# Scratch in DRAM as separate tiles, and the token-sum stores moved from SP's queue to GpSimd's, in a decoder trunk kernel

## The chip, the cores and the metric

The kernel runs on one core of a Trainium2 chip. The metric is the device time of one execution in microseconds (us); lower is better. The core's engines are TensorE (PE: matmuls and transposes), VectorE (DVE), ScalarE (ACT), GpSimd (POOL) and SyncE (SP, which here only issues transfers). Each engine works through its own instructions in the order in which the program issued them. A transfer (DMA) is issued from the queue of SP, ScalarE or GpSimd and runs on the core's 16 DMA engines; an instruction that touches its data waits for it by a semaphore.

## The reference

Two layers on 2048 tokens of width 1024, in float32. Only what the kernel's stages need is shown.

```python
def even_layer(h, positions, w_in, conv_w, conv_b, gn, w_out):
    q, k, v, g_ret, cb, cc, cx, g_conv = split_cols(h @ w_in, EVEN_SPLITS)
    ...
    r = retention(q, k, v)
    r = rms_norm(r, gn.reshape(RET_HEADS, RET_DV)).reshape(b, s, RET_V)
    y_conv = cb * short_conv(cc * cx, conv_w, conv_b)
    mix = jnp.concatenate([r * jax.nn.silu(g_ret), y_conv * jax.nn.silu(g_conv)], axis=-1)
    return mix @ w_out

def odd_layer(h, positions, w_in, q_a_norm, w_qb, kv_a_norm, w_kvb, w_out):
    cq, ckv, k_rope, gate = split_cols(h @ w_in, ODD_SPLITS)
    ...
    o = causal_mla_attention(q_nope, q_rope, k_nope, k_rope, v)
    return (o.reshape(b, s, MLA_V) * jax.nn.silu(gate)) @ w_out

def reference(x, positions, pre_norm, post_norm, ...):
    h = x
    for layer in range(DEPTH):
        u = rms_norm(h, pre_norm[layer])
        y = even_layer(u, ...) if layer % 2 == 0 else odd_layer(u, ...)
        h = h + rms_norm(y, post_norm[layer])
    return h
```

## The kernel before

The large products (input projection of the even layer, its output projection, the gate of the odd layer) are done by a fast matrix algorithm: a 2 x 2 block product becomes seven products P1 to P7 whose operands are blocks or sums of blocks. Each product is one **slot**: 12 matmuls on TensorE (three per 128 rows, on high and low parts of float32 numbers), about 2.7 us. Blocks are numbered by Q, seven slots each; Q from RQ=32 on is the convolution's input, from CE=64 on the output projection, from YE=80 on the gate.

The order of the work is written out by hand, slot by slot. In slot t the program issues: the small TensorE jobs of that slot (transposes) whose PSUM results are copied out at the slot's end; then `prep`, which loads a product's stationary operand eight slots ahead into a ring of nine tiles `us` (SP's queue), rounds it five slots ahead (ScalarE, line 327) and forms the low part four slots ahead (VectorE, line 335); then the list of events that were entered for the slot with `at(slot, f)`, in the order of their entry; then ScalarE's copies of the product's PSUM. Nothing is reordered later, so the place of an event in a slot is its place in its engine's queue.

Moving operands stand in wider tiles `u` (c4T and c4B by the program's names for the tiles that they lie in): `comb_dma` loads them (SP, line 348 for blocks from ub2_d, whose name in the trace is ub_d), `comb_split` rounds and splits them (ScalarE line 363, VectorE line 364).

Sums of blocks and other intermediate results lie in DRAM scratch tensors: one tensor each, whose first index is a token half, a head, a group of weights or a block of tokens. mix_d holds the mixed rows: index 0 the retention heads (stored by ScalarE), index 1 the convolution channels (stored by GpSimd, line 960, from a tile that the trace calls j). ms_d, gs_d, ws_d, s_d hold sums of four blocks, formed in two tiles jc (load by SP at line 424, four GpSimd operations, store by SP). tu_d and ub2_d hold the normed tokens of the odd layer, as sums and as blocks, for the gate's products.

The stage that the change touches runs beside the second half of the output projection. Tokens come in eight pairs w of tiles of 128, tA = 2w (even) and tB = 2w+1 (odd). A pair begins at slot n, and the next pair begins seven slots later, so two pairs overlap. For each tile (tB first, tA two slots later): `y_rstd` (ScalarE's sum of squares, then yss on GpSimd, lines 1048 and 1049), `y_h` (VectorE: h = x + normed y), `h_out` (GpSimd's store of h_d, line 1058), `y_rstd` again, `y_u2` (VectorE: yu, line 1061), `y_tr` (TensorE's eight transposes, up_tr, line 1071; ScalarE's copies of them into uo[h], line 1079, with two stores to ub2_d from ScalarE's queue, line 1080). Then for the pair: `y_sum` (four GpSimd subtractions in place in the two tiles uo, line 1090, two at slot n+13 and two at n+14), and `t_out`: four stores of a half of uo each to tu_d, in the order T3, T2 (these read uo[1]), T1, T4 (these read uo[0]), by SP at slot n+15 (line 1096). There is one tile uo for even and one for odd tokens, so the next pair's copies overwrite what the subtractions and stores read. `x_in` (SP, line 1099) loads x into the tile that h_out reads.

The events are entered in this loop:

```python
for t, o in ((tB, 0), (tA, 2)):
    ...
    at(n + 5 + o, lambda t=t: h_out(t))
    at(n + 6 + o, lambda t=t: y_rstd(t, 1, yb["x"][t % 2]))
    at(n + 7 + o, lambda t=t: y_u2(t))
    small(n + 9 + o, *y_tr(t))
for i in range(4):
    at(n + 13 + i // 2, lambda w=w, i=i: y_sum(w, i))
at(n + 15, lambda w=w: t_out(w))
```

Slot n+14 of a pair is slot n+7 of the next one, in which that one's h_out of its even tile is entered behind it.

Of the kernel before, what the change touches and what calls it, by code (L numbers as in the profile page):

```python
# [20 lines left out]
P = 128  # L21
# [43 lines left out]
def body(ctx, tc, x, positions, pre_norm, post_norm, w_heads, w_conv, even_conv_w, even_conv_b, ret_gn,  # L65
# [37 lines left out]
    ty_d = dram.tile([2, P, 4, 4, 512], F32, name="ty_d")  # L103
    wo_d = dram.tile([2, 2, 2, P, 4, 512], F32, name="wo_d")
    ms_d = dram.tile([16, P, 4, 512], F32, name="ms_d")
    gs_d = dram.tile([4, P, 4, 512], F32, name="gs_d")
    wg_d = dram.tile([8, 2, P, 512], F32, name="wg_d")
# [4 lines left out]
    a_d = dram.tile([8, P, 4, 512], F32, name="a_d")  # L112
    s_d = dram.tile([8, P, 4, 512], F32, name="s_d")
    wt_d = dram.tile([4, P, 4, 4, 384], F32, name="wt_d")
    uc_d = dram.tile([2, P, 4, 4, 512], F32, name="uc_d")
    wh_d = dram.tile([HR, 2, P, 1536], F32, name="wh_d")
    wc_d = dram.tile([32, 2, P, 512], F32, name="wc_d")
    ws_d = dram.tile([16, P, 4, 512], F32, name="ws_d")

# [63 lines left out]
    with ExitStack() as es:  # L183
# [96 lines left out]
        def mix_rows(q_, kh, t):  # L280
            return mix_d[q_, t, kh].rearrange("p k t -> p (k t)")

        def item_dma(n_):
            if n_ >= len(SEQ) or SEQ[n_] is None:
                return
            Q, p_ = SEQ[n_]
            i = LOF[p_]
            if Q < 8:
                return
            t_ = ring_tile(n_)  # L290
            ring[n_] = t_
            L = f32(t_[:, 1])
            if Q < RQ:
                u = Q % 8
                src = a_d[u, :, AIX[i]] if i in AIX else s_d[u, :, (SIX0 if u < 2 else SIX)[i]]
                SP.dma_start(flat(L), src)
            elif Q >= YE:
                c2 = (Q - YE) % 4
                if i in AIX:
                    r, kh = divmod(AIX[i], 2)  # L300
                    SP.dma_start(flat(L), wg_d[2 * c2 + r, kh])
                else:
                    SP.dma_start(flat(L), gs_d[c2, :, SIX0[i]])
            elif Q >= CE:
                q_, w = divmod(Q - CE, 8)
                if i in AIX:
                    r, kh = divmod(AIX[i], 2)
                    SP.dma_start(flat(L), mix_rows(q_, kh, 2 * w + r))
                else:
                    SP.dma_start(flat(L), ms_d[Q - CE, :, SIX0[i]])  # L310
            else:
                g, ct, w = CQ[Q - RQ]
                if i in AIX:
                    r, kh = divmod(AIX[i], 2)
                    SP.dma_start(flat(L), wc_d[COFF[w][r] * 8 + ct, kh])
                else:
                    SP.dma_start(flat(L), ws_d[2 * ct + w, :, SIX0[i]])

# [19 lines left out]
        def comb_dma(G_, n_):  # L338
            comb_new(G_, n_)
            for H, L, k0, nk in comb[G_][n_]:  # L340
                L = f32(L)
                if n_ in TIX:
                    src = (wt_d[G_] if G_ < 4 else uc_d[G_ - 4] if G_ < 6 else ty_d[G_ - 6] if G_ < 8 else tu_d[G_ - 8])[:, TIX[n_]]
                    SP.dma_start(flat(L), src[:, k0:k0 + nk].rearrange("p k c -> p (k c)"))
                elif G_ > 5:
                    j, h = int(n_[1]) - 1, int(n_[2]) - 1
                    src = wo_d[G_ - 6, j, h] if G_ < 8 else ub2_d[G_ - 8, h, j]
                    SP.dma_start(flat(L), src[:, k0:k0 + nk].rearrange("p k c -> p (k c)"))
                elif G_ < 4:
                    SP.dma_start(flat(L), wh_d[2 * G_ + int(n_[2]) - 1, int(n_[1]) - 1])  # L350
                else:
                    j, tb = int(n_[1]) - 1, 2 * (G_ - 4) + int(n_[2]) - 1
                    for uu in range(2):
                        for c in range(2):
                            o = (2 * uu + c) * P
                            SP.dma_start(L[:, :, o:o + P], a_d[2 * tb + uu, :, 2 * c + j, k0 * P:(k0 + nk) * P].rearrange("p (k c) -> p k c", k=nk))

# [55 lines left out]
        def job(kind, a, b, t_):  # L413
# [28 lines left out]
            def store():  # L442
                if kind in "wmg":
                    dst = {"w": ws_d, "m": ms_d, "g": gs_d}[kind]
                    SP.dma_start(dst[a].rearrange("p z c -> p (z c)"), t_.rearrange("p z c -> p (z c)"))
                elif kind == "y":
                    SP.dma_start(ty_d[a, :, :, b, :], t_)
                elif kind == "r":
                    SP.dma_start(wt_d[a, :, :, b, :], t_)
                else:  # L450
                    SP.dma_start(uc_d[a, :, :, b, :], t_)

# [11 lines left out]
        with ExitStack() as rs_:  # L464
# [175 lines left out]
            def mix_tr(v, pt):  # L640
                lo = 0 if v[0] is not None else 2
                hi = 4 if v[1] is not None else 2
                mxo = bp.tile([P, 4, P], F32, tag="mxo", bufs=1, name=f"mxo{v[0]}_{v[1]}")
                A.copy(mxo[:, lo:hi], pt[:, lo:hi, :])
                for i, s in enumerate(v):
                    if s is not None:
                        h, u = units[s]
                        A.dma_start(mix_d[0, 2 * u:2 * u + 2, h // 4, :, h % 4, :].rearrange("c p t -> p c t"), mxo[:, 2 * i:2 * i + 2])

# [125 lines left out]
            for hp in range(1, 4):  # L775
                for i, (h, j) in enumerate(((2 * hp, 0), (2 * hp, 1), (2 * hp + 1, 1))):
                    at(T0(8 * hp) - 40 + 6 * i, lambda h=h, j=j: SP.dma_start(wh_d[h, j], w_heads[h, j]))
            for q_ in range(16):
                g_, ct, w = CQ[q_]
                o0, o1 = (o * 8 + ct for o in COFF[w])  # L780
                at(T0(RQ + q_) - 25, lambda o0=o0: SP.dma_start(wc_d[o0], w_conv[o0]))
                at(T0(RQ + q_) - 22, lambda o1=o1: SP.dma_start(wc_d[o1, 1], w_conv[o1, 1]))

# [138 lines left out]
            def conv_engine(t_):  # L922
# [3 lines left out]
                if j < 5:  # L926
# [24 lines left out]
                    else:  # L951
# [111 lines left out]
            def y_tr(t):  # L1063
# [40 lines left out]
            for w in range(8):  # L1104
# [31 lines left out]
        with ExitStack() as cs_:  # L1136
# [31 lines left out]
    with ExitStack() as oes:  # L1168
# [26 lines left out]
        with ExitStack() as es:  # L1195
# [4 lines left out]
            with ExitStack() as es1:  # L1200
# [645 lines left out]
```

## Time and profile before

| | before |
|---|---|
| median of 3 runs (lowest to highest) | 3025.8 us (3025.24 to 3029.86) |
| profiled execution, its time and its span | 3029.42 us, 3027.6 us |
| TensorE busy | 2929.0 us (97%) |
| VectorE, ScalarE, GpSimd busy | 1998.2 (66%), 1506.9 (50%), 1112.2 us (37%) |
| mean granted TensorE clock | 0.99 |
| moved by DMA | 592.50 MB, mean 196 GB/s |
| of that by the hardware queues q1 and q10, and the software queue q0 | 496.89 MB, 28.08 MB, 64.50 MB |

The span is the time from the first to the last instruction of the profiled execution; the time of that execution is taken around it. Busy time is the sum of an engine's instructions, without those that only issue transfers from SP and ScalarE. A wait is idle time of an engine just before an instruction, put down to what released it last ("<- DVE yu" was released by VectorE's instruction that wrote yu). Engine names with a q (SPq, ACTq, PEld for TensorE's weight loads) stand for a queue of their own.

### The profile page before, as it was taken

What the parts mean: (1) busy time and instruction counts of PE and PEld (TensorE: products, weight loads), DVE (VectorE), ACT (ScalarE), POOL (GpSimd) and SP (SyncE); (2) the same over time, 40 slices, a digit from 0 to 9 for tenths busy, and PEclk for the clock granted to TensorE, in tenths of its full rate; (3) what the DMA queues carried; (4) which work ended last, traced back from release to release, by engine and by line L of the source; (5) the groups of instructions that cost most, each with busy time, mean ns of one, the idle gap of its engine ahead of it and who ended that gap; (6) DMA issues with size and microseconds to landing.
All of it is one profiled execution on the core that took longest, in us unless ns stands there. A gap on an engine that the chain in (4) does not pass through costs nothing.

```text
span 3027.6 us, 47252 instructions
## 1 busy us (share of the span) xinstructions
PE 2929.0 (97%) x16137; PEld 2568.8 (85%) x16137; DVE 1998.2 (66%) x3713; ACT 1506.9 (50%) x3596; POOL 1112.2 (37%) x1379
## 2 busy tenths in 40 slices
PE   7989999999999999999998899999999999999999
PEld 6878989898888888878886678988899999999887
DVE  7767777867565766684687754577666666666643
ACT  5645555556333533353565653333655555555521
POOL 5554454521442044534265400023333333334210
PEclk9999999999999999999999999999999999999999
DMA  7466777756887688799999875146111212211552
GB/s 294 164 241 204 235 250 249 245 166 202 300 301 235 208 303 293 267 335 308 345 294 315 278 246 153 58 159 207 59 61 60 66 53 62 63 59 58 171 169 89
DMA packets 364993, 592.50 MB, mean 196 GB/s; under 512 B 35568, under 2 KB 209280, under 8 KB 357248
## 3 DMA queue, kind: packets, MB, share of 16 engines
q1 hardware_dynamic: 292752, 496.89, 50.4%
q0 software_dynamic: 19184, 64.50, 5.9%
q10 hardware_dynamic: 52816, 28.08, 3.1%
q8 instruction: 128, 2.10, 0.3%
q14 instruction: 113, 0.93, 0.1%
HBM read 404.80 MB, written 213.65 MB: 204 GB/s over the span
## 4 chain that ended last, share of the span: by engine, by line
PE 82%; DMA 6%; DVE 3%; POOL 3%; ACT 2%; issue 2%; SPq 0%; ACTq 0%; POOLq 0%; DVEq 0%
PE bx L87 8%; PE bx L88 7%; PE bx L89 7%; PE fy L1788 5%; PE by L87 4%; PE by L88 4%; PE by L89 4%; PE T L1593 4%; PE o L1623 2%; PE o L1622 2%; PE o L1621 2%; PE S L1540 2%; PE S L1543 2%; PE S L1544 2%; PE S L1541 2%
## 5 line engine op out<-in xcount | busy, mean ns | idle before, releaser
L335 DVE TENSOR_TENSOR us<-us 128x512 fp32r<-128x512 f32 x560 | 463.0, 833 | 58.5 <-ACT us L327 55.6
L327 ACT CAST us<-us 128x512 fp32r<-128x512 f32 x560 | 338.3, 620 | 162.8 <-DMA us<-s_d 27.2
L1561 POOL TENSOR_SCALAR P<-P,al 128x512 f32<-128x512 f32 (+2 forms) x320 | 220.1, 698 | 353.6 <-DVE al L1566 168.9
L1551 ACT ACTIVATE P<-S,nm 128x512 f32<-128x512 f32 (+2 forms) x320 | 201.0, 628 | 197.6 <-DVE nm L1548 175.5
L1548 DVE TENSOR_REDUCE nm<-S 128x1 f32<-128x512 f32 (+2 forms) x320 | 194.2, 608 | 70.9 <-PE S L1544 43.0
L402 ACT COPY u<-bx 128x512 f32<-128x512 f32 (+1 forms) x172 | 94.1, 547 | 293.5 <-PE bx L89 293.0
L408 POOL TENSOR_TENSOR jc<-jc 128x512 f32<-128x512 f32 x138 | 198.6, 1439 | 39.6 <-DMA jc<-in_even_w_out 18.0
L1597 DVE TENSOR_TENSOR TL<-T,TH 128x512 fp32r<-128x512 f32 x224 | 154.3, 689 | 63.7 <-ACT TH L1596 62.6
L1621 PE MATMUL o<-TH,vH 128*128 128x256 f32 x576 | 185.3, 322 | 0.0
L1593 PE MATMUL T<-ident,P 128*128 128x128 f32 x1088 | 166.1, 273 | 0.0
L1623 PE MATMUL o<-TH,vL 128*128 128x256 f32 x576 | 162.7, 283 | 0.0
L1622 PE MATMUL o<-TL,vH 128*128 128x256 f32 x576 | 162.2, 282 | 0.0
L87 PE MATMUL bx<-c4T,us 128*128 128x512 f32 x384 | 150.5, 392 | 2.8 <-ACT u L402 2.0
L88 PE MATMUL bx<-c4T,us 128*128 128x512 f32 x384 | 149.7, 390 | 1.5 <-DVE c4T L364 1.5
L89 PE MATMUL bx<-c4T,us 128*128 128x512 f32 x384 | 149.5, 389 | 0.0
L1596 ACT CAST TH<-T 128x512 fp32r<-128x512 f32 x224 | 131.3, 586 | 24.1 <-PE T L1593 18.8
L1593 PEld LDWEIGHTS T<-ident,P 128*128 128x128 f32 x1088 | 125.1, 140 | 7.8
L1540 PE MATMUL S<-kH,aqn 128*128 128x512 f32 (+2 forms) x320 | 118.4, 370 | 0.1
L1543 PE MATMUL S<-K,aqr 128*128 128x512 f32 (+2 forms) x320 | 115.5, 361 | 0.0
L1541 PE MATMUL S<-kL,aqn 128*128 128x512 f32 (+2 forms) x320 | 115.3, 360 | 0.0
L1544 PE MATMUL S<-K,aqr 128*128 128x512 f32 (+2 forms) x320 | 115.2, 360 | 0.0
L1542 PE MATMUL S<-kH,aqn 128*128 128x512 f32 (+2 forms) x320 | 115.0, 359 | 0.0
(525 smaller groups left out, 9253.0 us busy)
## 6 DMA issues: line engine op xcount, KB each, us to landing
us<-ws_d SPq DMA_DIRECT2D x128, 256.0 KB, 4.7
us<-s_d SPq DMA_DIRECT2D x96, 256.0 KB, 5.0
us<-wc_d SPq DMA_DIRECT2D x96, 256.0 KB, 4.8
us<-a_d SPq DMA_DIRECT2D x72, 256.0 KB, 4.8
jc<-mix_d SPq DMA_DIRECT2D x64, 256.0 KB, 5.7
ms_d<-jc SPq DMA_DIRECT2D x16, 1024.0 KB, 6.8
us<-ms_d SPq DMA_DIRECT2D x64, 256.0 KB, 6.0
qn_d<-qn POOLq DMA_DIRECT2D x32, 512.0 KB, 3.4
```

What stands on the lines that cost most here:

```text
L87: PE.matmul(o, ah, bh, start=first, stop=False, **kw)
L88: PE.matmul(o, ah, bl, start=False, stop=False, **kw)
L89: PE.matmul(o, al, bh, start=False, stop=last, **kw)
L327: A.copy(ring[n_][:, 0], f32(ring[n_][:, 1]))
L335: V.tensor_tensor(out=t_[:, 1], in0=src, in1=f32(t_[:, 0]), op=ALU.subtract)
L408: sub = lambda o, a, b: (lambda: G.tensor_tensor(out=t_[:, o], in0=t_[:, a], in1=t_[:, b], op=ALU.subtract))
L1551: later(D_EXP, lambda: A.activation(p_[:, 0:w], sp[:, 0:w], AF.Exp, bias=nm[:, j:j + 1], accum_out=sm[:, j:j + 1]))
L1561: G.tensor_scalar(t_[:, 0:ww], t_[:, 0:ww], al[:, jj:jj + 1] if n > 1 else al[:, 5:6], al[:, 5:6] if n > 1 else 1.0, op0=ALU.mult, op1=ALU ...
L1593: PE.transpose(tp[:, e, z, :], src, ident)
L1621: PE.matmul(hold[i], vH[h][:, kb, :], pth[:, c], start=first, stop=False)
L1622: PE.matmul(hold[i], vH[h][:, kb, :], ptl[:, c], start=False, stop=False)
L1623: PE.matmul(hold[i], vL[h][:, kb, :], pth[:, c], start=False, stop=last)
```

## The change

Fifteen kinds of scratch tensor that were one DRAM tile with a leading index become a Python list of DRAM tiles, one for each value of that index; sizes, layouts within a part, and the transfers' shapes are the same. In addition `t_out` issues its four stores from GpSimd's queue instead of SP's, and is entered one slot earlier, at n+14, which puts it behind the last two subtractions and ahead of the next pair's h_out. The other tensors (a_d, s_d, wt_d, uc_d, wh_d, ws_d, wo_d, wg_d, gs_d, ty_d) are changed as the ones shown.

```diff
-    mix_d = dram.tile([2, NT, 2, P, 4, P], F32, name="mix_d")
+    mix_d = [dram.tile([NT, 2, P, 4, P], F32, name=f"mix_d{i}") for i in range(2)]
...
-    ub2_d = dram.tile([2, 2, 2, P, 4, 512], F32, name="ub2_d")
-    tu_d = dram.tile([2, P, 4, 4, 512], F32, name="tu_d")
+    ub2_d = [dram.tile([2, 2, P, 4, 512], F32, name=f"ub2_d{i}") for i in range(2)]
+    tu_d = [dram.tile([P, 4, 4, 512], F32, name=f"tu_d{i}") for i in range(2)]
...
-    ms_d = dram.tile([16, P, 4, 512], F32, name="ms_d")
+    ms_d = [dram.tile([P, 4, 512], F32, name=f"ms_d{i}") for i in range(16)]
...
-    wc_d = dram.tile([32, 2, P, 512], F32, name="wc_d")
+    wc_d = [dram.tile([2, P, 512], F32, name=f"wc_d{i}") for i in range(32)]
...
-                    SP.dma_start(flat(L), ms_d[Q - CE, :, SIX0[i]])
+                    SP.dma_start(flat(L), ms_d[Q - CE][:, SIX0[i]])
...
-                            G.dma_start(mix_d[1, n0:n0 + 4, ct // 4, :, ct % 4, :].rearrange("c p t -> p c t"), ah.rearrange("p (c t) -> p c t", c=4))
+                            G.dma_start(mix_d[1][n0:n0 + 4, ct // 4, :, ct % 4, :].rearrange("c p t -> p c t"), ah.rearrange("p (c t) -> p c t", c=4))
...
-                        A.dma_start(ub2_d[half, h, j][:, :, w * P:(w + 1) * P], uo[:, j * 512:(j + 1) * 512].rearrange("p (k t) -> p k t", k=4))
+                        A.dma_start(ub2_d[half][h, j][:, :, w * P:(w + 1) * P], uo[:, j * 512:(j + 1) * 512].rearrange("p (k t) -> p k t", k=4))
...
-                    SP.dma_start(tu_d[half, :, TIX[n_], :, w * P:(w + 1) * P], src.rearrange("p (k t) -> p k t", k=4))
+                    G.dma_start(tu_d[half][:, TIX[n_], :, w * P:(w + 1) * P], src.rearrange("p (k t) -> p k t", k=4))
...
-                at(n + 15, lambda w=w: t_out(w))
+                at(n + 14, lambda w=w: t_out(w))
```

## Rows read from the trace of the kernel before

**Rows 1.** windows: length, busy PE PEld DVE ACT POOL, clock, DMA share, GB/s

```profile
...
700.00:1300.00 600.00, 599.75 (x2678) 495.26 (x2677) 384.07 (x526) 241.85 (x439) 219.24 (x190) 1.00 0.81 267
1540.00:1720.00 180.00, 156.98 (x708) 125.25 (x707) 141.48 (x139) 113.31 (x260) 105.82 (x114) 0.97 0.93 310
...
```

**Rows 2.** waits of TensorE, 1540 to 1780: total us, times, longest

```profile
...
PE up_tr L1071 <- DVE yu L1061: 6.6, 4, 2.5
PE by L88 <- DVE c4B L364: 5.2, 1, 5.2
PE bx L87 <- ACT u L402: 4.9, 3, 2.6
...
```

**Rows 3.** waits of SP's queue, 1540 to 1730: total us, times, longest

```profile
...
SPq L1096 <- POOL uo L1090: 20.5, 16, 3.2
...
SPq L1096 <- POOL yss L1048: 16.1, 5, 4.5
SPq L348 <- DMA ub_d<-uo: 11.7, 3, 6.3
...
SPq L1099 <- DMA h_d<-yx: 6.8, 4, 2.2
...
```

**Rows 4.** timeline of POOL, 1590 to 1609: start, us, operation, idle before

```profile
...
1591.23 2.66 POOL L1090 TENSOR_TENSOR uo<-uo 128x512 f32<-128x512 f32 x2 [3.65 <-DMA ub_d<-uo]
...
1594.77 2.94 POOL L1090 TENSOR_TENSOR uo<-uo 128x512 f32<-128x512 f32 x2
1597.65 0.63 POOL L1058 DMA_DIRECT2D h_d<-yx  x1
...
1600.31 0.56 POOL L1049 TENSOR_TENSOR yss<-yss,nhalf 128x1 f32<-128x1 f32 x1
...
```

**Rows 5.** timelines of VectorE and TensorE, two stretches each, columns as above

```profile
...
1600.90 1.78 DVE L1061 TENSOR_SCALAR yu<-yx,yss 128x1024 f32<-128x1024 f32 x1 [0.73 <-POOL yss L1049]
...
1603.04 0.60 PE L1071 MATMUL up_tr<-ident,yu 128*128 128x128 f32 x4
...
1646.86 1.78 DVE L1061 TENSOR_SCALAR yu<-yx,yss 128x1024 f32<-128x1024 f32 x1 [0.73 <-POOL yss L1049]
...
1650.63 0.60 PE L1071 MATMUL up_tr<-ident,yu 128*128 128x128 f32 x4
...
```

**Rows 6.** timelines of ScalarE, 1590 to 1609 and 1640 to 1680

```profile
...
1597.37 1.14 ACT L1079 ACTIVATE uo<-up_tr,gcol 128x128 f32<-128x128 f32 x4 [5.51 <-PE up_tr L1071]
...
1603.72 1.15 ACT L1079 ACTIVATE uo<-up_tr,gcol 128x128 f32<-128x128 f32 x4
1605.54 0.52 ACTq L1080 DMA_DIRECT2D ub_d<-uo  x1
...
1653.74 1.05 ACT L363 CAST u<-u 128x1024 fp32r<-128x1024 f32 x1 [4.64 <-DMA u<-ub_d]
...
```

**Rows 7.** tensor mix_d over the span: ns min/median/max, first and last start

```profile
...
L424 SPq DMA_DIRECT2D jc<-mix_d x64: 319/432/2905, 1109.5 to 1456.5; - x64
...
L960 POOL DMA_DIRECT2D mix_d<-j x32: 750/770/1017, 756.8 to 1345.3; - x32
...
```

**Rows 8.** timelines of SP's queue, 1590 to 1609 and 1640 to 1657

```profile
...
1593.91 4.18 SPq L1096 DMA_DIRECT2D tu_d<-uo  x4
...
1603.28 0.33 SPq L1099 DMA_DIRECT2D yx<-in_x  x1
...
1639.88 4.19 SPq L1096 DMA_DIRECT2D tu_d<-uo  x4
...
1644.71 0.83 SPq L348 DMA_DIRECT2D u<-ub_d  x1
...
```

**Rows 9.** DMA issues: count, KB each, median us from issue to landing

```profile
...
mix_d<-j POOLq DMA_DIRECT2D x32, 256.0 KB, 5.6
...
tu_d<-uo SPq DMA_DIRECT2D x32, 256.0 KB, 2.8
...
```

**Rows 10.** line 960: all its DMAs, min/median/max us from issue to landing

```profile
...
DMA to landing us min/median/max: 3.4/5.6/9.2
```

More of the change, by code (lines that the diff above doesn't have):

```diff
@@ L97, in body @@
     dram = ctx.enter_context(tc.tile_pool(name="dram", bufs=1, space=DRAM))
-    mix_d = dram.tile([2, NT, 2, P, 4, P], F32, name="mix_d")
+    mix_d = [dram.tile([NT, 2, P, 4, P], F32, name=f"mix_d{i}") for i in range(2)]
     h_d = dram.tile([S, D], F32, name="h_d")
     yp_d = dram.tile([S, D], F32, name="yp_d")
-    ub2_d = dram.tile([2, 2, 2, P, 4, 512], F32, name="ub2_d")
-    tu_d = dram.tile([2, P, 4, 4, 512], F32, name="tu_d")
-    ty_d = dram.tile([2, P, 4, 4, 512], F32, name="ty_d")
-    wo_d = dram.tile([2, 2, 2, P, 4, 512], F32, name="wo_d")
-    ms_d = dram.tile([16, P, 4, 512], F32, name="ms_d")
-    gs_d = dram.tile([4, P, 4, 512], F32, name="gs_d")
-    wg_d = dram.tile([8, 2, P, 512], F32, name="wg_d")
+    ub2_d = [dram.tile([2, 2, P, 4, 512], F32, name=f"ub2_d{i}") for i in range(2)]
+    tu_d = [dram.tile([P, 4, 4, 512], F32, name=f"tu_d{i}") for i in range(2)]
+    ty_d = [dram.tile([P, 4, 4, 512], F32, name=f"ty_d{i}") for i in range(2)]
+    wo_d = [dram.tile([2, 2, P, 4, 512], F32, name=f"wo_d{i}") for i in range(2)]
+    ms_d = [dram.tile([P, 4, 512], F32, name=f"ms_d{i}") for i in range(16)]
+    gs_d = [dram.tile([P, 4, 512], F32, name=f"gs_d{i}") for i in range(4)]
+    wg_d = [dram.tile([2, P, 512], F32, name=f"wg_d{i}") for i in range(8)]
     gate_d = dram.tile([D, S], F32, name="gate_d")
@@ L111, in body @@
     qr_d = dram.tile([HM, P, S], F32, name="qr_d")
[L112 to L116, printed above, removed]
-    wc_d = dram.tile([32, 2, P, 512], F32, name="wc_d")
-    ws_d = dram.tile([16, P, 4, 512], F32, name="ws_d")
+    a_d = [dram.tile([P, 4, 512], F32, name=f"a_d{i}") for i in range(8)]
+    s_d = [dram.tile([P, 4, 512], F32, name=f"s_d{i}") for i in range(8)]
+    wt_d = [dram.tile([P, 4, 4, 384], F32, name=f"wt_d{i}") for i in range(4)]
+    uc_d = [dram.tile([P, 4, 4, 512], F32, name=f"uc_d{i}") for i in range(2)]
+    wh_d = [dram.tile([2, P, 1536], F32, name=f"wh_d{i}") for i in range(HR)]
+    wc_d = [dram.tile([2, P, 512], F32, name=f"wc_d{i}") for i in range(32)]
+    ws_d = [dram.tile([P, 4, 512], F32, name=f"ws_d{i}") for i in range(16)]
     const = ctx.enter_context(tc.tile_pool(name="const", bufs=1))
@@ L280, in mix_rows @@
         def mix_rows(q_, kh, t):
-            return mix_d[q_, t, kh].rearrange("p k t -> p (k t)")
+            return mix_d[q_][t, kh].rearrange("p k t -> p (k t)")
         def item_dma(n_):
@@ L294, in item_dma @@
                 u = Q % 8
-                src = a_d[u, :, AIX[i]] if i in AIX else s_d[u, :, (SIX0 if u < 2 else SIX)[i]]
+                src = a_d[u][:, AIX[i]] if i in AIX else s_d[u][:, (SIX0 if u < 2 else SIX)[i]]
                 SP.dma_start(flat(L), src)
@@ L300, in item_dma @@
                     r, kh = divmod(AIX[i], 2)
-                    SP.dma_start(flat(L), wg_d[2 * c2 + r, kh])
+                    SP.dma_start(flat(L), wg_d[2 * c2 + r][kh])
                 else:
-                    SP.dma_start(flat(L), gs_d[c2, :, SIX0[i]])
+                    SP.dma_start(flat(L), gs_d[c2][:, SIX0[i]])
             elif Q >= CE:
@@ L314, in item_dma @@
                     r, kh = divmod(AIX[i], 2)
-                    SP.dma_start(flat(L), wc_d[COFF[w][r] * 8 + ct, kh])
+                    SP.dma_start(flat(L), wc_d[COFF[w][r] * 8 + ct][kh])
                 else:
-                    SP.dma_start(flat(L), ws_d[2 * ct + w, :, SIX0[i]])
+                    SP.dma_start(flat(L), ws_d[2 * ct + w][:, SIX0[i]])
         def item_hi(n_):
@@ L346, in comb_dma @@
                     j, h = int(n_[1]) - 1, int(n_[2]) - 1
-                    src = wo_d[G_ - 6, j, h] if G_ < 8 else ub2_d[G_ - 8, h, j]
+                    src = wo_d[G_ - 6][j, h] if G_ < 8 else ub2_d[G_ - 8][h, j]
                     SP.dma_start(flat(L), src[:, k0:k0 + nk].rearrange("p k c -> p (k c)"))
                 elif G_ < 4:
-                    SP.dma_start(flat(L), wh_d[2 * G_ + int(n_[2]) - 1, int(n_[1]) - 1])
+                    SP.dma_start(flat(L), wh_d[2 * G_ + int(n_[2]) - 1][int(n_[1]) - 1])
                 else:
@@ L355, in comb_dma @@
                             o = (2 * uu + c) * P
-                            SP.dma_start(L[:, :, o:o + P], a_d[2 * tb + uu, :, 2 * c + j, k0 * P:(k0 + nk) * P].rearrange("p (k c) -> p k c", k=nk))
+                            SP.dma_start(L[:, :, o:o + P], a_d[2 * tb + uu][:, 2 * c + j, k0 * P:(k0 + nk) * P].rearrange("p (k c) -> p k c", k=nk))
         def comb_split(G_, n_, half, sub=V):
@@ L446, in store @@
                 elif kind == "y":
-                    SP.dma_start(ty_d[a, :, :, b, :], t_)
+                    SP.dma_start(ty_d[a][:, :, b, :], t_)
                 elif kind == "r":
-                    SP.dma_start(wt_d[a, :, :, b, :], t_)
+                    SP.dma_start(wt_d[a][:, :, b, :], t_)
                 else:
-                    SP.dma_start(uc_d[a, :, :, b, :], t_)
+                    SP.dma_start(uc_d[a][:, :, b, :], t_)
             return [load] + job_ops(t_, kind) + [store]
@@ L647, in mix_tr @@
                         h, u = units[s]
-                        A.dma_start(mix_d[0, 2 * u:2 * u + 2, h // 4, :, h % 4, :].rearrange("c p t -> p c t"), mxo[:, 2 * i:2 * i + 2])
+                        A.dma_start(mix_d[0][2 * u:2 * u + 2, h // 4, :, h % 4, :].rearrange("c p t -> p c t"), mxo[:, 2 * i:2 * i + 2])
             NU = len(units)
@@ L776, in body @@
                 for i, (h, j) in enumerate(((2 * hp, 0), (2 * hp, 1), (2 * hp + 1, 1))):
[L777 removed]
+                    at(T0(8 * hp) - 40 + 6 * i, lambda h=h, j=j: SP.dma_start(wh_d[h][j], w_heads[h, j]))
             for q_ in range(16):
@@ L781, in body @@
                 at(T0(RQ + q_) - 25, lambda o0=o0: SP.dma_start(wc_d[o0], w_conv[o0]))
-                at(T0(RQ + q_) - 22, lambda o1=o1: SP.dma_start(wc_d[o1, 1], w_conv[o1, 1]))
+                at(T0(RQ + q_) - 22, lambda o1=o1: SP.dma_start(wc_d[o1][1], w_conv[o1, 1]))
             x_load(0)
@@ L811, in t_op @@
                     V.tensor_tensor(out=raw0[o][:, c], in0=raw0[a_][:, c], in1=raw0[b_][:, c], op=ALU.subtract)
-                SP.dma_start(wt_d[0, :, TIX[n_]].rearrange("p k c -> p (k c)"), raw0[o])
+                SP.dma_start(wt_d[0][:, TIX[n_]].rearrange("p k c -> p (k c)"), raw0[o])
             rope_pos(psb)
@@ L1155, in body @@
                     if (ct % 2, kh) != (1, 0):
-                        at(T0(CE) + 2 + 7 * ct + kh, lambda ct=ct, kh=kh: SP.dma_start(wg_d[ct, kh], w_gate[ct, kh]))
+                        at(T0(CE) + 2 + 7 * ct + kh, lambda ct=ct, kh=kh: SP.dma_start(wg_d[ct][kh], w_gate[ct, kh]))
             at(T0(CE) + 6, y_open)
@@ L1225, in u_dma @@
                         w = (t % 8) // 2
-                        SP.dma_start(urr[t][:, 4 * j:4 * j + 4, :], ub2_d[t // 8, t % 2, j][:, :, w * P:(w + 1) * P])
+                        SP.dma_start(urr[t][:, 4 * j:4 * j + 4, :], ub2_d[t // 8][t % 2, j][:, :, w * P:(w + 1) * P])
                 def u_split(t):
```

2 lines of the change are left out of this document (1 added, 1 removed).

## The prediction

> **What bounds the kernel now.** I read the page first: TensorE is busy 97% of the span, so time comes or goes only where TensorE waits, or is made to. The table by stretches says where that is [rows 1]. From 700 to 1300 us TensorE is busy 599.75 us of 600, though the DMA engines are busy 0.81 of the time there; from 1540 to 1720, the stage in which the changed stores lie, it is busy 156.98 us of 180, at a granted clock of 0.97 and a DMA share of 0.93. So 23 us of idling stand in that stage, and the reader is to see that nothing is idle where most of the split tiles (mix_d, ws_d, wc_d, a_d) are at work.
>
> The table of waits tells what TensorE waits for in the stage [rows 2]. The largest is the transposes of a normed tile (up_tr, line 1071) waiting for VectorE's last scaling (yu, line 1061): 6.6 us in four waits. Then two sorts that belong to the combined operand tiles loaded in the same slots: 5.2 us for c4B, 4.9 us for ScalarE's copies of u (line 402). The rest is smaller.
>
> Then SP's queue, which issues every operand load [rows 3]: in front of the four token-sum stores (line 1096) it stood 20.5 us in 16 waits for GpSimd's subtractions, and 16.1 us in 5 more. The loads queued behind were late by as much. That is what the move to GpSimd takes off SP, and the case for it.
>
> Last, timelines of one pair of token tiles, engine by engine, to see in which order the work goes. GpSimd subtracts twice at 1591.23 and twice at 1594.77, then at once issues the hidden-state store h_d at 1597.65 in 0.63 us, and has at 1600.31 the small power (yss) that VectorE's scaling of 1600.90 is waiting for [rows 4, 5]. TensorE transposes its result at 1603.04, 0.36 us after the scaling's end at 1602.68. ScalarE copies the other tile's transposes out at 1597.37, this one's at 1603.72 to 1604.87, and issues the store of its halves at 1605.54 [rows 6]; the next pair's first subtractions wait for such a store.
>
> **Part 1: the split of the scratch tensors.** It takes away a wait only if a load now waits for a store to another index of the same tensor. mix_d is the test: its loads (line 424) begin at 1109.5 us while stores of line 960 to the other half go on to 1345.3 [rows 7]. With a wait on the whole tensor the first load would have come after the last of these. Sizes, shapes and numbers of the transfers stay. So 0, and no work is needed to hide it. Below it, what a freed wait could be worth at most is the 11.7 us that SP waits for a store of ub_d in this stage [rows 3]: a load there reads the very pair that was stored, so I expect it to stay. Above it, nothing is added.
>
> **Part 2a: four DMA issues on GpSimd, in front of the next pair's work.** A pair's four stores are now issued after its fourth subtraction, ahead of h_out and of the yss of the next pair's even tile, in GpSimd's order. The nearest row is a GpSimd store of the same size and shape, mix_d from j: 750 to 1017 ns of the engine, median 770 [rows 7]; four are 3.08 us (3.0 to 4.1). yss, VectorE's scaling and the transposes come that much later; behind the scaling VectorE has its operand splits, and behind the transposes TensorE has its main products. What covers it is the slack at the transposes: 0.36 us in the pair shown, from 1602.68 to 1603.04. Of the six pairs that run in this loop four look like that (slack 0.35, 0.36, 0.36, 0.61) and two like the one at 1640: the scaling ends at 1648.64, the transposes begin at 1650.63, slack 1.99 (the other 2.28) [rows 5]. So TensorE is stopped for 2.5 + 3 x 2.7 + 1.1 + 0.8 = 12.5 us over the stage.
>
> **Part 2b: the stores land later, and ScalarE waits for them.** A store reads half of the tile that ScalarE fills next. T3 is now issued by SP at 1593.91, right after the first two subtractions, and is over when ScalarE starts at 1597.37 [rows 6, 8]. Moved behind all four subtractions it can't start before 1597.65, and ScalarE must wait until it has landed. SP's stores of tu_d land 2.8 us after the issue; GpSimd's of the same size land after a median of 5.6, 3.4 at the least and 9.2 at the most [rows 9, 10]. I take 4.2, midway between 2.8 and 5.6: the destination is that of the SP row, the queue that of the other. ScalarE's copy starts 1597.65 + 4.2 − 1597.37 = 4.5 us late. The slack that eats it is that before its stores: the copies of the even tile end at 1604.87, the store is issued at 1605.54, 0.67 us [rows 6]; in the four early pairs this is 0.67, 2.06, 0.67 and 0.75. The lateness passes from there round the loop: store, next pair's subtractions, yss, scaling, transposes. This is the same path as 2a's, so the greater of the two counts in each pair: 4.0 − 0.67 = 3.3, 2.7 (2a's), 4.5 − 0.67 = 3.8, 4.5 − 0.75 = 3.7 (the first pair's start of copies lies 0.2 us after its subtractions, the others' 0.3 before). The last two pairs have ScalarE late for other reasons, so 2a's 1.1 and 0.8 stay. The sum is 15.4 us. With 2.8 us to landing only 2a is left, 12.5; with 9.2 the four pairs cost about 8 to 9 each, some 35 in all.
>
> **Part 2c: what SP gains.** SP no longer stands from 1593.91 to 1598.09 in line 1096, nor in the wait ahead of it; loads behind go out sooner. In the later pairs one of them matters: u from ub_d was issued at 1644.71 right behind the stores that ended at 1644.07, and ScalarE waited 4.64 us for it [rows 6, 8]. TensorE's own 4.9 us of waits for such copies [rows 2] is the most that this returns on that side; I take 2, since SP's next wait, a load of x into the tile that h_out is still reading (6.8 us in four [rows 3]), grows as h_out moves back by 3.08 us. The DMA engines, 0.93 busy here, carry the same bytes.
>
> **Sum.** 15.4 − 2 = +13.4 us. The profiled execution took 3029.42 us for a span of 3027.6, 3.6 us above the median of 3025.8; the change is put on the median: 3039. Its own range goes from 12.5 − 6.6 = +6, where the new stops only take the place of the waits for yu of today, to +35 (3032 to 3061).
>
> On the choice of queue, the rows set 770 ns of GpSimd's time per store against stores on SP, an engine that computes nothing. The Trainium skill ("DMA: Bandwidth & Descriptors", section "SWDGE vs HWDGE vs iDMA") puts plain transfers on SP or ScalarE and leaves GpSimd those that cast, accumulate or are irregular. Under "Issuing engines are not separate DMA queues" it adds that a second issuing engine saves only sequencer time. By that the gain of 2c would be all there is to win, and the trace agrees in so far as all tu_d bytes stay.
>
> **Rivals.** *Hidden anyway* (no change, 3020 to 3032). With a DMA share of 0.93 [rows 1] the loads may be what sets the pace; then a stop of TensorE lets loads catch up, and later waits shrink by as much. For it: 10.1 us of waits on operand tiles stand in the stage. Against: 12.5 us must be swallowed with only 6.6 + 10.1 there to swallow it. It decides where less than half gets through: 3026 ± 6.
>
> *SP was the trouble* (faster). SP gets the 36.6 us of [rows 3] back, loads go out earlier, and the waits for operand tiles, 5.2 + 4.9 [rows 2], go away, while the stores' cost hides behind the slack: 3025.8 − 10 = 3016. It decides where the four issues on GpSimd take under the slack, about 0.1 us each instead of 0.77, and T3 lands within the 2.8 of SP's. Against it: line 960's issues never took less than 750 ns.
>
> *The split frees a wait.* If SP's 11.7 us on ub_d is a wait for another index after all, up to that much comes back: about 3018 with the rest neutral. Against: mix_d [rows 7]. That the split does nothing is in my sum already.
>
> *A store that VectorE holds up.* GpSimd's issue could be stopped for as long as a VectorE instruction lasts that runs over it, 1.78 us for line 1061 [rows 5]: four of them are 7.1 us a pair on top, some 35 more in five pairs, 3075. The longest GpSimd store of line 960 took 1.02 us beside a busy VectorE, and that speaks against it. The Trainium skill ("SBUF — State Buffer", section "SBUF: two separate sides") has this rule: descriptors of a DMA issued by GpSimd can't be written while VectorE holds the shared port pair. By the rule the issues would stretch wherever VectorE's scalings run; the trace of before doesn't show it.
>
> **Numbers.** My forecast has 0.62; hidden 0.17; SP 0.13; the split 0.04; held-up stores 0.04. Two runs of this kernel can't be told apart within 0.2%, 6 us. Faster 0.13 + 0.04 = 0.17, same 0.17, slower 0.62 + 0.04 = 0.66. The range of 3018 to 3056 leaves out half of the case for SP and the split, the held-up stores, and the end of mine above +30 (a landing time that only the longest of 32 stores showed), together 0.2.
>
> **What would show it.** In the changed profile's GpSimd timeline four tu_d DMAs stand between the last subtraction and h_out, near 0.77 us each (2a); the waits of up_tr for yu exceed 6.6 us (2a); ScalarE's copies into uo wait for a landing of tu_d, by 3 to 5 us in the early pairs (2b); SP's waits at line 1096 are gone and that for h_d is above 6.8 (2c); TensorE's busy time from 700 to 1300 stays within 1 us of 599.75 (part 1). I am wrong if the issues take far less than 0.7 us, if the stores land within 3 us, or if TensorE's idle time in the stage doesn't grow beyond 23 us.

## The result, and the profile after

The changed kernel takes 3049.23 us (median of 4 runs, 3047.17 to 3050.49) against 3027.83 us of the kernel before, run again beside it (4 runs): ratio 1.0064, 95% interval 1.0051 to 1.0077. The medians lie 21.4 us apart; the interval allows 15 to 23. The forecast was slower, +13.4.

Since both kernels do the same products in the same order, stages can be compared product by product, wherever they lie in time. Two stretches matter: the **loop**, the 28 slots from 515 on in which the pairs of tokens follow each other, and the **second stretch**, the 17 slots behind it, in which the gate's operand tiles are loaded as well. First the two stretches in the kernel before, then in the changed one, with a stretch far from the change ahead of them (columns as in [rows 1]).

```profile
...
1553.70:1647.90 94.20, 86.82 (x402) 70.45 (x402) 72.66 (x69) 57.80 (x140) 61.41 (x70) 0.98 0.91 305
1647.90:1720.60 72.70, 57.06 (x246) 43.91 (x245) 56.91 (x60) 47.28 (x103) 32.29 (x33) 0.95 0.95 322
...
```

```profile
...
700.00:1300.00 600.00, 599.81 (x2675) 495.39 (x2674) 381.03 (x523) 241.89 (x439) 219.14 (x192) 1.00 0.80 266
1550.80:1656.30 105.50, 90.89 (x402) 70.83 (x401) 77.75 (x68) 56.11 (x136) 73.42 (x85) 0.97 0.82 270
1656.30:1739.50 83.20, 63.45 (x246) 48.15 (x245) 59.19 (x62) 51.43 (x114) 39.82 (x47) 0.88 0.87 293
...
```

The same 402 and 246 matmuls took 94.2 and 72.7 us before and take 105.5 and 83.2 now: +11.3 and +10.5, together 21.8, and that is the whole loss (the two profiled spans differ by 19.9). TensorE's idle time went from 7.4 to 14.6 us and from 15.6 to 19.8, its busy time from 86.8 to 90.9 and from 57.1 to 63.5. Nothing was added to its work: the granted clock fell from 0.98 to 0.97 and from 0.95 to 0.88. From 700 to 1300 us TensorE is as busy as in [rows 1].

Next GpSimd's timeline of one pair in the changed kernel, the counterpart of [rows 4].

```profile
...
1592.22 3.50 POOL L1090 TENSOR_TENSOR uo<-uo 128x512 f32<-128x512 f32 x2
...
1597.79 2.98 POOL L1090 TENSOR_TENSOR uo<-uo 128x512 f32<-128x512 f32 x2
1600.70 3.08 POOL L1096 DMA_DIRECT2D tu_d<-uo  x4
1603.78 0.55 POOL L1058 DMA_DIRECT2D h_d<-yx  x1
...
1606.00 0.56 POOL L1049 TENSOR_TENSOR yss<-yss,nhalf 128x1 f32<-128x1 f32 x1
...
```

The four stores stand where they were put: behind the last subtractions, 3.08 us long, ahead of h_out and of the yss that ends at 1606.56. ScalarE in the same pair, and two pairs later (counterpart of [rows 6]):

```profile
...
1597.89 0.61 ACT L327 CAST us<-us 128x512 fp32r<-128x512 f32 x1
1606.51 1.14 ACT L1079 ACTIVATE uo<-up_tr,gcol 128x128 f32<-128x128 f32 x4 [8.01 <-DMA tu_d<-uo]
...
1612.70 1.14 ACT L1079 ACTIVATE uo<-up_tr,gcol 128x128 f32<-128x128 f32 x4
...
```

```profile
...
1650.78 0.60 ACT L327 CAST us<-us 128x512 fp32r<-128x512 f32 x1
1661.41 1.14 ACT L1079 ACTIVATE uo<-up_tr,gcol 128x128 f32<-128x128 f32 x4 [10.03 <-DMA tu_d<-uo]
1662.59 0.52 ACTq L1080 DMA_DIRECT2D ub_d<-uo  x1
...
```

```profile
...
ACT uo L1079 <- DMA tu_d<-uo: 33.4, 4, 10.0
...
```

The copies into uo start 5.81 us after T3's issue at 1600.70, and ScalarE stood 8.01 us for its landing where it stood 5.51 us for TensorE before [rows 6]. In the pair behind the loop it stood 10.03 us. Four such waits are 33.4 us; before they were 9.6. Two more, of 7.89 and 9.85 us, are put down to other engines, but the copies start 0.1 to 0.2 us after T3's landing there too. Then the waits of TensorE and of SP's queue, and the stores themselves:

```profile
...
PE up_tr L1071 <- DVE yu L1061: 10.9, 8, 2.2
PE bx L87 <- ACT u L402: 8.0, 5, 2.6
...
PE up_tr L1071 <- ACT uo L1079: 3.5, 1, 3.5
...
PE up_sk L1071 <- ACT uo L1079: 1.9, 4, 0.9
...
```

```profile
...
SPq L1099 <- DMA h_d<-yx: 57.5, 11, 10.5
...
SPq L1099 <- DVE yu L1061: 16.6, 5, 3.9
...
```

```profile
...
tu_d<-uo POOLq DMA_DIRECT2D x32, 256.0 KB, 5.3
...
```

```profile
...
L1096 POOL DMA_DIRECT2D tu_d<-uo x32: 750/752/842, 1547.8 to 1747.6; - x32
...
```

The wait for yu is 10.9 us where it was 6.6 [rows 2]. New is TensorE's wait for ScalarE: the transposes of the second tile can't go into up_tr until the first tile's are copied out. SP no longer waits at line 1096 (36.6 us in [rows 3]), but at line 1099 in front of x: 57.5 us for h_d, where it was 6.8, and 16.6 for VectorE (2.3 before). The stores cost GpSimd 752 ns each and land after 5.3 us.

Last the clock, in TensorE's timeline around the pair at 1661 and in stretches of 3 us:

```profile
...
1658.74 0.39 PE L89 MATMUL bx<-row,us 128*128 128x512 f32 x1
1662.61 1.00 PE L1071 MATMUL up_tr<-ident,yu 128*128 128x128 f32 x4 [3.48 <-ACT uo L1079]
...
1666.25 0.63 PE L89 MATMUL ba<-c4T,us 128*128 128x512 f32 x1
...
1669.24 0.57 PE L87 MATMUL ba<-row,us 128*128 128x512 f32 x1
...
1669.87 0.39 PE L89 MATMUL ba<-row,us 128*128 128x512 f32 x1
...
```

```profile
...
1656.00:1659.00 3.00, 3.00 (x14) 2.25 (x12) 0.32 (x1) 0.00 (x0) 2.81 (x5) 1.00 0.97 255
1659.00:1662.00 3.00, 0.13 (x1) 0.00 (x0) 2.52 (x3) 0.59 (x3) 1.68 (x2) 1.00 1.04 405
1662.00:1665.00 3.00, 1.52 (x7) 1.12 (x8) 0.43 (x1) 1.70 (x7) 0.00 (x0) 0.63 1.02 374
1665.00:1668.00 3.00, 3.00 (x10) 2.43 (x9) 1.06 (x2) 2.98 (x5) 1.14 (x3) 0.50 0.81 242
1671.00:1674.00 3.00, 3.00 (x15) 2.44 (x13) 1.94 (x3) 2.41 (x6) 0.77 (x2) 1.00 0.95 305
...
```

TensorE stood from about 1659.1 to 1662.6. Its clock then reads 0.63 and 0.50, the lower of the two levels (1.2 GHz), and matmuls of 0.39 us take 0.63, one starting every 0.43 us instead of 0.23, until 1669. So the stop of 3.5 us was followed by some 2 us more of lost time.

### The profile page after: what moved, and what is told of

Same layout as the page of the kernel before. It is cut to its first block, busy times and chain, and to the rows that moved or that the text cites. A ratio compares the mean times of both kernels' runs of the same rounds, so it can differ in the third digit from the quotient of the medians.

```text
span 3047.5 us, 47244 instructions
## 1 busy us (share of the span) xinstructions
PE 2939.8 (96%) x16137; PEld 2574.7 (84%) x16137; DVE 1996.7 (66%) x3713; ACT 1506.3 (49%) x3596; POOL 1126.9 (37%) x1411
## 4 chain that ended last, share of the span: by engine, by line
PE 83%; DMA 5%; ACT 3%; DVE 3%; POOL 3%; issue 2%; ACTq 1%; SPq 0%; POOLq 0%; DVEq 0%
PE bx L87 8%; PE bx L88 8%; PE bx L89 8%; PE fy L1788 5%; PE by L87 4%; PE by L88 4%; PE by L89 4%; PE T L1593 4%; PE o L1623 2%; PE o L1622 2%; PE o L1621 2%; PE S L1540 2%; PE S L1543 2%; PE S L1544 2%; PE S L1541 2%; PE S L1542 2%
## 5 line engine op out<-in xcount | busy, mean ns | idle before, releaser
L335 DVE TENSOR_TENSOR us<-us 128x512 fp32r<-128x512 f32 x560 | 453.8, 816 | 61.9 <-ACT us L327 58.9
L1548 DVE TENSOR_REDUCE nm<-S 128x1 f32<-128x512 f32 (+2 forms) x320 | 194.1, 608 | 69.4 <-PE S L1544 41.9
```

The source lines that it names most:

```text
L335: V.tensor_tensor(out=t_[:, 1], in0=src, in1=f32(t_[:, 0]), op=ALU.subtract)
```

## The experiments

The theories. *Landing*: ScalarE's copies wait for T3, which starts too late. *Issue*: GpSimd's four issues ahead of yss are the cost. *SP*: what SP now waits for (h_d, in front of x) keeps back the loads. *Split*: the separate tiles themselves matter. The times of all runs, and the lengths of the two stretches in their traces (from the first matmul of slot 515 to that of 543, and on to that of 560). Each ratio is to the kernel before, run beside that kernel; e6 has two runs, the others four to twelve:

| kernel | median us | ratio to before (95%) | loop, us | second stretch, us |
|---|---|---|---|---|
| before, profiled; once more (e12) | 3027.59 | 0.9994 (0.9985 to 1.0002) | 94.2; 93.7 | 72.7; 74.5 |
| changed | 3049.23 | 1.0064 (1.0051 to 1.0077) | 105.5 | 83.2 |
| e1, split only | 3025.45 | 0.9984 (0.9975 to 0.9993) | 91.5 | 74.5 |
| e13, split only, again | 3024.72 | 0.9985 (0.9976 to 0.9994) | 89.8 | 74.5 |
| e10, a_d, s_d, wt_d, wh_d split | 3026.71 | 0.9989 (0.9978 to 0.9999) | 93.3 | 74.9 |
| e2, move only | 3050.23 | 1.0063 (1.0044 to 1.0081) | 106.1 | 81.4 |
| e3, T3 and T2 from another tile | 3035.23 | 1.0019 (1.0010 to 1.0029) | 94.6 | 78.7 |
| e4, stores behind yss | 3064.46 | 1.0109 (1.0093 to 1.0125) | 113.0 | 87.3 |
| e6, h_out first | 3059.42 | 1.0102 (1.0075 to 1.0128) | 111.7 | 87.1 |
| e11, SP, T3 late | 3048.48 | 1.0059 (1.0043 to 1.0074) | 107.0 | 82.6 |
| e5, ScalarE's queue | 3040.71 | 1.0038 (1.0023 to 1.0052) | 94.2 | 86.0 |
| e8, SP, T1 and T4 later | 3029.90 | 1.0002 (0.9992 to 1.0013) | 93.4 | 78.0 |
| e14, T3 and T2 on SP | 3035.55 | 1.0015 (1.0006 to 1.0024) | 91.3 | 79.3 |

**e1 and e2: the two parts alone.** The diff is e1's, against the changed kernel; e2 has the same two lines the other way round, against the kernel before.

```diff
-                    G.dma_start(tu_d[half][:, TIX[n_], :, w * P:(w + 1) * P], src.rearrange("p (k t) -> p k t", k=4))
+                    SP.dma_start(tu_d[half][:, TIX[n_], :, w * P:(w + 1) * P], src.rearrange("p (k t) -> p k t", k=4))
-                at(n + 14, lambda w=w: t_out(w))
+                at(n + 15, lambda w=w: t_out(w))
```

> Only the split: separate DRAM tiles, the token-sum stores left on SP at n+15. Theory landing (ScalarE's copies into uo wait for T3, which GpSimd issues late): no part in it, 3028 +- 5 us. Theory split (the separate tiles themselves cost the time, by their place in DRAM or by new waits): 3040 to 3050.

> Only the move: one DRAM tensor each, the four stores from GpSimd at n+14. Theory landing, and theory issue (four issues of 0.75 us stand ahead of yss in GpSimd's order): the whole loss, 3049 +- 5. Theory split: back at 3028.

The move alone makes the whole loss, the split none of it.

**e3: nothing that ScalarE overwrites is read by T3 and T2.**

```diff
                 a_, b_ = yb["o"]
+                if w2 < 7:
+                    b_ = yb["g"]
```

> The changed kernel, but in pairs 0 to 6 the stores T3 and T2 read the tile of the post-norm's weights and not uo[1], so tu_d holds other data in T3 and T2; place, size and number of the four GpSimd issues stay. Nothing that ScalarE overwrites is read by T3 any more. Theory landing: ScalarE's waits for tu_d fall from 33.4 us to under 5, the time to 3033 to 3041 (what the issues cost stays). Theory issue: 3047 to 3050, as changed. Theory SP (SP's waits of 57.7 us for h_d in front of x keep back the loads): over 3044, since h_out comes as late as before.

GpSimd's four issues, SP's and TensorE's waits in this kernel (its lines lie two further down from here on):

```profile
...
1593.87 1.60 POOL L1098 DMA_DIRECT2D tu_d<-yp  x2
1595.46 1.49 POOL L1098 DMA_DIRECT2D tu_d<-uo  x2
1596.94 0.55 POOL L1058 DMA_DIRECT2D h_d<-yx  x1
...
```

```profile
...
SPq L1101 <- DMA h_d<-yx: 67.5, 11, 11.4
...
```

```profile
...
PE up_tr L1071 <- DVE yu L1061: 11.2, 5, 2.2
...
```

The issues take 3.09 us as in the changed kernel and h_out is as late, and yet the loop is back at 94.6 us, 3 to 5 above the split alone. TensorE's wait for yu is 11.2 us, 4.6 above [rows 2]; 9.0 of it lie in the loop, where it was 6.6 before and is 4.0 to 4.7 with the split alone. It stands in another place: before, in front of the odd tile's transposes (first fence; the even tile's stand in [rows 5] without a wait); in e3, in front of the even tile's (second fence, second line).

```profile
...
1596.63 0.66 PE L1071 MATMUL up_tr<-ident,yu 128*128 128x128 f32 x4 [2.15 <-DVE yu L1061]
...
```

```profile
...
1592.85 0.65 PE L1071 MATMUL up_tr<-ident,yu 128*128 128x128 f32 x4
...
1601.65 0.63 PE L1071 MATMUL up_tr<-ident,yu 128*128 128x128 f32 x4 [2.24 <-DVE yu L1061]
...
```

So the stop that the issues make is there, 2.2 us a pair, but against the split alone about half of it takes the place of another. Of the 9.2 us that TensorE idles in the loop 9.0 are for yu, so SP's 67.5 us in front of x do not lengthen it. Issue falls as the main cause, but not to nothing: e3's median is still some 10 us above the split alone, 3 to 5 of them in the loop and 4 in the second stretch. There Issue and SP are not told apart.

**e4 and e6: other places in GpSimd's order.** In e4 t_out stands behind the next pair's yss, in e6 (n + 7 and + 21 in the diff) between its h_out and its yss.

```diff
-                at(n + 14, lambda w=w: t_out(w))
+                if w > 0:
+                    at(n + 8, lambda w=w: t_out(w - 1))
+            at(T0(CE + 15) + 22, lambda: t_out(7))
```

> The changed kernel with t_out entered one slot later, behind the next pair's h_out and yss of its even tile: yss no longer stands behind the four issues, and T3 starts some 3 us later. Theory issue: 3028 to 3033. Theory SP: h_out is back in its old place, 3030 to 3037. Theory landing: ScalarE's waits for tu_d grow by some 3 us in each of four or five pairs, 3055 to 3065.

> The changed kernel with the next pair's h_out entered ahead of the four stores on GpSimd. h_d goes out 3 us earlier, T3 0.6 us later. Theory SP (SP's waits of 57.7 us for h_d in front of x are what costs): these waits fall under 35 us and the time to 3030 to 3042. Theory landing: T3's landing sets the pace, 3048 to 3055.

ScalarE's waits in e4:

```profile
...
ACT uo L1079 <- DMA tu_d<-uo: 66.4, 8, 12.0
...
```

Both took yss or h_out away from behind the stores, both made T3 later, and both lost more: some 15 and 10 us on top of the change. e6 was expected at 3048 to 3055 by Landing and came out at 3059 (two runs): T3 not only started 0.6 us later, it also landed 6.2 to 6.6 us after its issue in the first four pairs, for 5.3 to 5.7 in the changed kernel, and a pair lasts 28.0 us against 26.4.

**e11: T3 late, on SP.** The split alone with the order of SP's stores turned round.

```diff
-                for n_, src in (("T3", b_[:, 0:512]), ("T2", b_[:, 512:1024]), ("T1", a_[:, 0:512]), ("T4", a_[:, 512:1024])):
+                for n_, src in (("T4", a_[:, 512:1024]), ("T1", a_[:, 0:512]), ("T3", b_[:, 0:512]), ("T2", b_[:, 512:1024])):
```

> The split alone, with SP's four stores in the order T4, T1, T3, T2: SP waits for the last subtraction first, so T3 starts some 4 us later than with the split alone, and GpSimd issues nothing more than before. Theory landing: ScalarE's copies wait for T3 again, some 3 us in each of the first four pairs (SP's stores land within 2.9 us, GpSimd's took 5.5), 3032 to 3042. Theory issue (GpSimd's four issues are the cost): as the split alone, 3022 to 3029.

SP's timeline, ScalarE's, the landing times, and SP's and TensorE's waits in the loop:

```profile
...
1604.56 3.30 SPq L1096 DMA_DIRECT2D tu_d<-uo  x4
...
```

```profile
...
1610.18 1.14 ACT L1079 ACTIVATE uo<-up_tr,gcol 128x128 f32<-128x128 f32 x4 [7.92 <-DMA tu_d<-uo]
...
```

```profile
...
tu_d<-uo SPq DMA_DIRECT2D x32, 256.0 KB, 4.4
...
```

```profile
...
SPq L1096 <- POOL uo L1090: 21.2, 4, 5.3
...
```

```profile
...
PE up_tr L1071 <- ACT uo L1079: 6.5, 4, 2.3
PE up_sk L1071 <- ACT uo L1079: 4.9, 4, 1.2
...
```

This is the decisive run. GpSimd issues nothing more than before, SP hardly waits for h_d (2.0 us), and the loss is that of the change: 3048.48. ScalarE stands 7.92 us where the changed kernel has 8.01. Nor does SP stand longer at its stores in the loop: 21.2 us, with the split alone 21.6 to 22.5; and TensorE waits there for ScalarE's copies out of up_tr and up_sk and for yu (2.2 us), not for an operand load. In the second stretch SP does stand longer at the stores, 11.5 us for 4.5 to 5.5, and its share there is not told apart. The expectation of 3032 to 3042 was too low; it took SP's stores to land in 2.9 us: four that go out within 3.30 us land in 4.4 (median), four spread over the subtractions (e13) in 2.8.

**e5: ScalarE's queue.**

```diff
-                    G.dma_start(tu_d[half][:, TIX[n_], :, w * P:(w + 1) * P], src.rearrange("p (k t) -> p k t", k=4))
+                    A.dma_start(tu_d[half][:, TIX[n_], :, w * P:(w + 1) * P], src.rearrange("p (k t) -> p k t", k=4))
-                at(n + 14, lambda w=w: t_out(w))
+                at(n + 15, lambda w=w: t_out(w))
```

> The changed kernel with the four token-sum stores issued from ScalarE's queue at n+15. GpSimd's order is that of before; T3 is issued before the last subtractions are through and should land before ScalarE copies into uo. Theory landing: no waits of ScalarE for tu_d beyond those of the kernel with the split alone, 3022 to 3034 (four issues of about 0.5 us on ScalarE against SP's waits). If the move off SP was worth nothing in itself it isn't under 3022; if SP's waits at these stores had been a cost, 3010 to 3020.

```profile
...
1589.09 5.40 ACTq L1096 DMA_DIRECT2D tu_d<-uo  x4
1594.54 1.06 ACT L1047 ACTIVATE yu<-yx 128x1024 f32<-128x1024 f32 x1 [6.33 <-POOL uo L1090]
...
```

The loop is 94.2 us, near the split's, as Landing has it. But the second stretch is 86.0: ScalarE is now held by its own stores, from 1589.09 on for 5.40 us, until GpSimd has subtracted, and the rounding of operand tiles stands behind it. The expected time was missed by 7 us. SP computes nothing and holds back only loads when it waits in order; ScalarE holds back its own work.

**e8 and e14: half of the stores elsewhere.** T3 and T2 stay on SP at n+15; T1 and T4 go out on SP at n+16 (e8) or on GpSimd at n+14 (e14, whose diff is shown; a second argument of t_out picks the half).

```diff
+                at(n + 14, lambda w=w: t_out(w, 1))
                 at(n + 15, lambda w=w: t_out(w))
```

> The split, all four stores on SP, T3 and T2 at n+15 and T1 and T4 one slot later at n+16, so that SP doesn't stand in front of T4 for the last subtraction. Theory landing: T3 lands as early as with the split alone, SP waits some 10 us less at line 1096, and the time is that of the split alone within 5 us (3020 to 3030). If SP's waits cost time, under 3020.

> The split, with T3 and T2 (what ScalarE overwrites next) left on SP at n+15 and only T1 and T4 issued from GpSimd at n+14. Theory landing: T3 lands early, so the time of the split alone, 3021 to 3030; if SP's shorter standing is worth something, under 3021. Theory issue: two issues, 1.5 us ahead of yss in each pair, half of the loss, 3032 to 3040.

Both keep the loop short (93.4, 91.3), as Landing has it, and neither is faster than the split alone. In e8 SP's waits for GpSimd at line 1096 did not shrink as expected: 35.6 us, with the split alone 32.7 and 35.1. In e14 they fell to 23.8, and SP's waits for h_d in front of x grew to 41.9, from 9.2 to 9.4 (24.2 in e8); most of these lie in the loop, which stays short. e14's time, 3035.55, is in Issue's range and misses Landing's. But the loop, where Issue would show, is the split's; in the profiled executions e14 is slower by 2.5 to 4.3 us before slot 515, by 4.8 in the second stretch, and by 4.2 to 5.2 behind slot 560. What costs it there stays open.

In the second stretch e8 and e14 are slower than the split alone by 3.5 and 4.8 us. A wait for h_d of 5.5 and one of 9.7 us reach into it (0.8 to 1.1 with the split alone), and the gate's operand loads stand behind them; but ScalarE also stands longer for a landing of tu_d there, 7.9 and 8.0 us for 5.4 to 6.0. That fits SP as a smaller second cause, and Landing as well; no run took either away alone.

**e10, e12, e13: is the split worth anything?** e10 splits a_d, s_d, wt_d and wh_d only; e12 is the kernel before, e13 is e1 again.

> The kernel before with only a_d, s_d, wt_d and wh_d held as separate tiles (those that work in the first 560 us), stores on SP at n+15. If the 4 us that the split alone gained are a wait or a placement in that stage: 0.9975 to 0.9992 of the time before. If they are spread over the program, or are no effect of the split: 0.9992 to 1.0008.

> The kernel before, unchanged, timed against itself: shows how far two samples of one kernel lie apart. 0.9990 to 1.0010 of the time before.

> The split alone once more, with more rounds. If the split itself gains: 0.9975 to 0.9993 of the time before, and the first 500 us shorter by 2 us or more than in the kernel before profiled beside it. If the 4 us were chance: 0.9993 to 1.0007.

Three samples with the split lie below the time before, with intervals that exclude no change; the kernel before against itself gave 0.9994, with an interval that doesn't. From the first product to slot 162 the three traces without the split took 506.6, 508.9 and 504.1 us (e2), the eleven with it 500.8 to 506.1, median 502.7. So some 3 to 5 us (0.1 to 0.16%) are likely the split's, in the first 550 us and before any of the moved stores; but the two sets overlap, and so do the intervals of e10 and e13 and that of e12. Which wait or placement brings it stays open.

## Why the prediction was right, and where its sum was not

The direction and the place were right: slower, in the stage of the normed tokens, through GpSimd's order and ScalarE's wait for T3. That the sum came within 8 us is in part luck: 13.5 us of it were for the four early pairs, that is the loop, which grew by 11.3; 1.9 were for the last two, and the second stretch, in which they lie, grew by 10.5. The steps:

- **Part 1, the split, 0.** TensorE's busy time from 700 to 1300 stayed (599.81), and so did SP's wait for ub_d (11.1 and 11.5 us with the split alone). A gain of some 4 us early on, under what was called measurable, was not foreseen.
- **Part 2a, 12.5 us: the cost right, its effect too large.** An issue took 752 ns for 770 forecast, and e3 has the stops where the text put them, 2.2 us at the even tile for 2.7. But the stops at the odd tiles went at the same time, so that the loop is 3 to 5 us longer than the split's. The text had this as the low end of its own range (the new stops take the place of today's) and did not choose it. Nor do the issues set the pace: e11 has none of them and the whole loss.
- **Part 2b: right in mechanism, too small in the last two pairs.** It was to add 2.9 us to 2a's; e3, which takes it away, is 14 us faster than the changed kernel, the greater part of the loss. T3's landing was put at 4.2 us, midway; it was 5.3 in the median and 5.4 to 5.8 from issue to copy in the four pairs of the loop. For the last two pairs the text said that ScalarE is late for other reasons, and added nothing; there it stood longest, 10.03 and 9.85 us, where before it had stood 5.77 and 5.55. This is the step that left most out. On the other side ScalarE had been waiting 5.51 us for TensorE anyway, so that 8.01 us of waiting lengthened a pair by about 2.5, not by the 3.3 to 3.8 forecast: from 1539.33 to 1645.08 the subtractions of five pairs begin 26.4 us apart on average, before from 1542.3 to 1637.2 it was 23.7.
- **The clock was not in the sum.** Of the 21.8 us, 11.3 are idle time of TensorE and 10.5 are the same matmuls taking longer, at a clock of 0.97 and 0.88. The second part changes from execution to execution: in e12, the kernel before, TensorE is busy 60.4 us in the second stretch, not 57.1, at a clock of 0.91, and against that trace it is 7.7 us. The Trainium skill ("TensorE: Matmul & The Clock Gate", section "Part 1: The HAM clock gate") says that full speed is what activity earns and that an array that has not been busy runs at the lower rate. The trace agrees: after the stop at 1659 the clock read 0.50.
- **Part 2c, −2 us: nothing came back.** SP's 36.6 us at line 1096 became 74.1 at line 1099; the text had SP's wait for h_d grow only with h_out's 3.08 us. TensorE's 4.9 us of waits for ScalarE's copies of u are 8.0 now. e14, with some 10 us less of SP's waits at these stores, is not faster either.
- **The rivals.** Hidden anyway: no. SP was the trouble: no; an issue took 750 ns, and no kernel in which SP stands less at these stores (changed, e3, e5, e14) is faster than before. The split frees a wait: a gain of some 4 us, but SP's wait for ub_d stayed, and the cause is open. A store held up by VectorE: not in the changed kernel, where the longest of 32 issues took 842 ns; a scaling of line 1061 ran beside only two of them. The Trainium skill ("SBUF — State Buffer", section "SBUF: two separate sides") has descriptors of GpSimd's DMAs wait while VectorE holds the shared port pair. e4 agrees: five of its stores are issued just as a scaling starts, and took 1137 to 1142 ns. The trace of before has one such case too, an h_d store of 1.02 us beside a scaling, where the median is 0.63; the text says that it shows none. At 0.39 us a pair this is too small for the loss.

Of the kernels run the split alone is the fastest, 3024.72 and 3025.45 us, and beats both, the kernel before by 0.15%.

## What to carry to other kernels

Before a store is moved, ask who overwrites what it reads and when: its start and its landing matter to that engine, and the queue's cost per issue may matter less. Put the store that the next writer waits for first. An engine relieved of one wait in an ordered queue goes on to the next one in it; see what that is, and who stands behind it, before counting the time as won.

## What was not expected of the hardware

Four stores of 256 KB landed after 2.8 us (median) when SP issued them between subtractions, after 4.4 when SP issued them within 3.30 us, and after 5.3 from GpSimd within 3.08 us. So the same queue gave both a fast and a slow landing. That the burst alone makes the difference is not shown: in e5 four stores spread over 5.40 us from ScalarE's queue landed after 5.5, in e8 two and two from SP after 4.7.

After a stop of TensorE of 3.5 us the clock read 0.50, and 0.39 us matmuls lasted 0.63 us for some 4 us.

VectorE's scaling (line 1061) and GpSimd hold each other up. First GpSimd, then VectorE, in e4 (of the four stores at 1606.25 the first took 1.14 us, the others 0.75):

```profile
...
1600.16 2.97 POOL L1090 TENSOR_TENSOR uo<-uo 128x512 f32<-128x512 f32 x2
...
1606.25 3.38 POOL L1096 DMA_DIRECT2D tu_d<-uo  x4
...
```

```profile
...
1600.22 1.78 DVE L1061 TENSOR_SCALAR yu<-yx,yss 128x1024 f32<-128x1024 f32 x1 [0.44 <-POOL yss L1049]
...
1606.32 0.75 DVE L1061 TENSOR_SCALAR yu<-yx,yss 128x1024 f32<-128x1024 f32 x1 [0.73 <-POOL yss L1049]
...
```

Over all traces the scaling took 1.74 to 1.79 us in the 174 cases in which GpSimd had begun an operation on 128x512 elements just before it, and 0.74 to 0.87 in the other 50. In the loop it is nearly always the long one, since GpSimd goes on to such an operation right behind the yss that the scaling waits for. So about 1 us of the way from yss to the transposes lies there; no run took it away.
